# A one-core encoder layer: order of work in the opening, at three stage borders and in the last output tile

## Chip, core and metric

The kernel runs on one core of one Trainium2 chip. The metric is the device time of one execution in microseconds (us). Engines are called PE (matrix multiply; PEld is its weight load), DVE (vector), ACT (scalar), POOL (GpSimd) and SP (the queue that issues every DMA here). L331 is line 331 of the kernel before.

## What is computed

One layer of a bidirectional hybrid encoder on 1024 tokens plus 16 meta tokens, width 1024, all in float32:

```
h    = rmsnorm(concat(meta, x))
q,k,v,z,beta,a,scB,scC,scX,gateA,gateB = split(h @ w_in)      # 9248 columns
q,k,v = silu(conv5(q,k,v));  q,k l2-normalised per head       # 8 heads of 128
g    = -exp(A_log) * softplus(a + dt_bias)                    # log decays, per token, direction, head
o    = gated delta rule, chunks of 64, forward + backward     # needs cumulative sums of g
yA   = (rmsnorm(o) * silu(z)) @ w_branch_dn
yB   = (scB * conv3(scC * scX)) @ w_branch_sc
x    = h_in + (sigmoid(gateA) * yA + sigmoid(gateB) * yB) @ w_out
x    = x + (silu(gate) * up) @ w_down,  gate,up = rmsnorm(x) @ w_gate_up
out  = rmsnorm(x), meta tokens dropped
```

## The kernel before

**Products.** Every large product is taken in three parts: each operand is split into a high part (ACT casts it, L86) and a low part (DVE subtracts, L87), and PE adds high*high, high*low and low*high in one PSUM bank. So each new operand costs one ACT and one DVE instruction ahead of its matmuls. Eight PSUM banks are shared under three tags (m: 3, e: 2, d: 3).

**Opening and phase 1 (to about 1005 us).** This part runs in the order in which the source issues it; that order is partly written out by hand and partly dealt by a planner in the source with a model clock per engine (`T["pe"]`, `T["dve"]`, ...). Nine tiles of x are loaded, scaled (`root`, `scaled`, L1020) with the norm row `w1row`, turned on PE (`turned`, L83) and split (`highs`, `lows`). Between these steps the first two units of the input projection, `gen0` (K of head 0) and `gen1` (Q of head 0), are issued piece by piece: a unit is 128 columns of w_in against all tokens in three column chunks (`dense_steps`, L331), each chunk evicted by ACT (L387, L388) into a row buffer `ra` (two of them) for the convolution, which DVE does (`conv_job`, L354, L362, with a tanh on ACT, L359). A unit may evict into a row buffer only when the convolution of the unit two before it has read it. `small_gates` (L1051) multiplies the 32 columns of beta and a, whose split weights are `wba` (L1116 on ACT, L1118 on DVE). At the end of the opening the last pieces of `gen0` and `gen1` and the last `small_gates` are issued, and only then the last chunks of both units are evicted, the third unit (V of head 0) is picked and its weights are split in four pieces (`split_part`, L942 on ACT, L939 on DVE). From there the main loop goes on unit by unit and lets the planner put other work between the matmuls: `g_gates` (decays and their cumulative sums; the sums are matmuls with triangular constants, L1261), then per head `g_decay`, `g_norm`, `g_inv` and `g_scan` (the recurrence).

**Stages after it.** Here the compiler's scheduler deals instructions to the engine queues, among ready ones the earlier in the source first; matmuls of one step can so stand between those of another. The gate A, short-conv and DeltaNet projections are each done by `seven`: seven half-size products A to G of four operand steps, alternating between two sets of four banks, with copies or an eviction after a product. `halved` splits one operand step into one of four buffer pairs. For the DeltaNet branch the eviction (`evict_dn`) has three DVE instructions for each of four tiles when a kept part is added, two when none is; it leaves the merged rows `mg` (tiles mA and mB). `between` lists hold work hooked between the operand steps, among it `wo_row` (load and split one row tile of w_out). Then a loop over eight token tiles splits `mg` into `mh, ml` and multiplies with w_out (L1584 to L1586), adds x, normalises, and turns the tile one step late (`norm_T`). The feed-forward part prepares three units ahead (`stationary1`: load and split of gate and up columns; `part1`: first two products, L1644 to L1646), with `norm_T` of the last tile and `split_T2` between the second and the third.

**The end.** The down projection is again seven products, over 11 steps each. In the last one, five operand steps are kept back and done tile by tile, and `finish` normalises each tile and stores it. A late tile is stored in two halves: the high half scaled by ACT from `hiw`, the low half by DVE.

Of the kernel before, what the change touches and what calls it, by code (L numbers as in the profile page):

```python
# [8 lines left out]
F32 = mybir.dt.float32  # L9
# [7 lines left out]
P = 128  # L17
# [20 lines left out]
def encoder_layer(ctx: ExitStack, tc: tile.TileContext, x, meta, norm1_w, w_in,  # L38
# [26 lines left out]
    def psd():  # L65
        return ps.tile([P, 512], F32, tag="e", name=uid("pe"), bufs=2)
# [921 lines left out]
    with tc.tile_pool(name="st", bufs=1) as st:  # L988
# [29 lines left out]
        def scaled(t):  # L1018
            p = size(t)
            nc.vector.scalar_tensor_tensor(out=xs[t][:p], in0=xs[t][:p], scalar=rss[t][:p, 1:2], in1=w1row[:p],  # L1020
                                           op0=ALU.mult, op1=ALU.mult)
# [35 lines left out]
        def steps(g, n=KT):  # L1057
            for _ in range(n):
                next(g)
# [5 lines left out]
                transpose(idle[:, :P], ident)  # L1065

        load(0)
        load(1)
        nc.sync.dma_start(w1row, norm1_w[0:1, :].broadcast_to([P, D]))
        load(2)  # L1070
        u0 = pick()
        load(3)
# [41 lines left out]
        nc.scalar.copy(cols[:, :24], pt2[:, :24])  # L1114
        nc.scalar.mul(cols[:, 24:25], pt2[:, 24:25], 0.5)
        nc.scalar.copy(wba[:, :, 0:32], raw_ba)  # L1116
        scaled(3)
        nc.vector.tensor_tensor(out=wba[:, :, 32:64], in0=raw_ba, in1=wba[:, :, 0:32].bitcast(F32), op=ALU.subtract)  # L1118
        nc.scalar.copy(u1[1][0], u1[2])
        nc.gpsimd.tensor_tensor(out=u1[1][1], in0=u1[2], in1=u1[1][0].bitcast(F32), op=ALU.subtract)  # L1120
        root(4)
# [36 lines left out]
        lows(8, 0)  # L1158
        lows(8, 1)
        steps(gen0)  # L1160
        steps(gen1)
        small_gates(2)


# [27 lines left out]
    def g_gates():  # L1192
# [4 lines left out]
        nc.sync.dma_start(dtb, dt_bias.rearrange("a b c -> a (b c)").broadcast_to([P, 16]))  # L1197
        nc.sync.dma_start(alg, A_log.rearrange("a b c -> a (b c)").broadcast_to([P, 16]))
        nc.gpsimd.memset(BA, 0.0)
        pba = psd()  # L1200
        pbm = psd()
        for c in range(9):
# [33 lines left out]
        for k in (13, 11, 9, 7, 5, 3, 1):  # L1236
# [6 lines left out]
        nc.vector.tensor_scalar(out=alg, in0=alg, scalar1=-1.0, scalar2=None, op0=ALU.mult)  # L1243
        g = sr
        nc.vector.scalar_tensor_tensor(out=g, in0=a_, scalar=0.0, in1=sr, op0=ALU.max, op1=ALU.add)
        nc.vector.tensor_tensor(out=g, in0=g, in1=alg.unsqueeze(1).broadcast_to([P, 9, 16]), op=ALU.mult)
# [3 lines left out]
        nc.gpsimd.affine_select(out=g[:, 8, :], in_=g[:, 8, :], compare_op=ALU.is_gt, fill=0.0,  # L1250
                                base=META, pattern=[[0, 16]], channel_multiplier=-1)
        gcs = [c1.tile([P, 8, 9], F32, name=f"gc{d}") for d in range(2)]
        yield T["dve"] + 700
        for d in range(2):
            nc.vector.tensor_copy(gcs[d].rearrange("p h c -> p c h"), g[:, :, d * 8:d * 8 + 8])
            small_v()
        yield T["dve"] + TOPE
        for d in range(2):
            pt = psd().rearrange("p (a n) -> p a n", a=4)
            for i, m in enumerate((U2[d], U[d], E_[d], ones)):  # L1260
# [34 lines left out]
    for m_ in meta_inv:  # L1295
        nc.gpsimd.memset(m_, 0.0)
    SPL = (4, 6, 8, 10)
    for g in (gen0, gen1):
        for _ in g:
            pass  # L1300
    decs.append([g_gates(), T["pe"], None])
    ahead = [pick(), pick()]
    ahead[0][1] = wtiles([P, KT, P])
    while done < H or qkv_units or fill_units or any(ahead):
        u = ahead.pop(0)
        if u is None:
# [60 lines left out]
    def seven(pairs, X, Y, tok, evict, between, moving={}, snap=snap):  # L1367

        p1s = u2s = p5s = None
        for n, (key, bank, first) in enumerate((("A", X, True), ("B", Y, True), ("C", X, False), ("D", Y, True),  # L1370
                                                ("E", X, False), ("F", Y, False), ("G", X, False))):
            for f in between[n][0]:
                f()
            for k in range(4):
                h_, l_ = halved(pairs[key], k, 512 if key in moving else D)
                bh, bl = moving[key](k) if key in moving else (h_[:, hi], l_[:, hi])
                for t in range(4):
                    c = slice(t * P, t * P + P)
                    for j, (a, b) in enumerate(((h_, bh), (h_, bl), (l_, bh))):
                        fresh = first and k == j == 0  # L1380
                        mm(bank[t], a[:, c], b, start=fresh, stop=first and k == 3 and j == 2,  # L1381
                           skip_group_check=not first)
                for f in between[n][1 + k]:
                    f()
            if n in (0, 2, 3):
                keep_ = snap(n)
                for t in range(4):
                    nc.scalar.copy(keep_[t], bank[t])
                if n == 0:
                    p1s = keep_  # L1390
                elif n == 2:
                    u2s = keep_
                else:
                    p5s = keep_
            elif n == 6:
                evict(1, tok[0], bank, None)
            else:
                evict(*((0, tok[0], bank, p1s), (1, tok[1], bank, p5s), (0, tok[1], bank, u2s))[(1, 4, 5).index(n)])

    def p_block(dst, kh, half):  # L1400
# [144 lines left out]
    def wo_row(j):  # L1545
        raw = s4(D)
        nc.sync.dma_start(raw, w_out[j * P:j * P + P, :])
        split(*(t[:, j % 4] for t in wo[j // 4]), raw)

    during_dn = [  # L1550
        [[lambda: (new("G", "ah1"), w_part("G", 1, 1))], [lambda: by_two(add, L_(dn_, "D"), L_(dn_, "C"), L_(dn_, "A"))], [],
         [lambda: by_two(sub, R_(dn_, "D"), R_(dn_, "F"), R_(dn_, "C"))], []],
# [3 lines left out]
        [[lambda: wo_tiles(0, ("b0", "b3"))], [lambda: wo_row(0)], [lambda: wo_row(1)], [lambda: wo_row(2)], []],  # L1556
        [[], [lambda: wo_row(3)], [lambda: wo_tiles(1, ("b2", "b1"))], [lambda: wo_row(4)], []],
        none,
        [[], [], [lambda: wo_row(5)], [lambda: wo_row(6)], [lambda: wo_row(7)]]]
    seven(dn_, bank_m, bank_d, (1, 0), evict_dn, during_dn)  # L1560
    woh, wol = ([wo[j // 4][i][:, j % 4] for j in range(KT)] for i in range(2))
    rot["i"] = 4

# [8 lines left out]
    m32 = [m_[0][:, 0:2], m_[0][:, 2:4], m_[1], m_[2]]  # L1572
    m32 = [m.rearrange("p k i c -> p (k i) c") for m in m32]
    for t in range(KT):
        mh, ml = wtiles([P, KT, P])
        for i in range(2):
            split(mh[:, 4 * i:4 * i + 4], ml[:, 4 * i:4 * i + 4], mg[i][:, :, t * P:(t + 1) * P])
        xr = s4(D)
        nc.sync.dma_start(xr, x[t * P:(t + 1) * P])
        for n in range(2):  # L1580
# [104 lines left out]
    mov["T1"] = [[t1s[2 * i + k // 2][:, k % 2] for k in range(4)] for i in range(2)]  # L1685
    ahead = [part1(w0, sm[:, 0], sm[:, 2])]
    ahead.append(part1(stationary1(1), sm[:, 1], sm[:, 3]))
    norm_T(*late_norm)
    split_T2(slice(384, 512))
    p1_2 = [tp.tile([P, 512], F32, tag="t2", name=uid("t2"), bufs=2) for _ in range(2)]  # L1690
    ahead.append(part1(stationary1(2), *p1_2))
    u_hl[0] = big("w2", [P, 2, 4, P])
    block22(0, w0[1], w0[2])
    for n, i in (("T3", 3), ("T4", 2), ("B22", 0)):
# [97 lines left out]
    def finish(t):  # L1792
# [14 lines left out]
        nc.vector.scalar_tensor_tensor(out=r[:, lo], in0=r[:, lo], scalar=ss[:, 2:3], in1=wfr[:, lo], op0=ALU.mult, op1=ALU.mult)  # L1807
        nc.sync.dma_start(o_[:, lo], r[:, lo])

    half_ss = {}  # L1810
    for n, (a, b, bank) in enumerate((("A11", "B11", bank_x), ("A12", "B21", bank_y), ("S2", "T2", bank_x), ("S1", "T1", bank_y),
                                      ("S3", "T3", bank_x), ("S4", "B22", bank_y), ("A22", "T4", bank_x))):
        kept = []
        for k in range(HK):
            hl = operands(a, b, k)
            if n == 6 and k >= HK - NR:
                kept.append((k, hl))
                continue
            for t in range(4):
                tile_step(bank, hl, t, k == 0, k == HK - 1)  # L1820
        for t in range(4):
            for k, hl in kept:
                tile_step(bank, hl, t, False, k == HK - 1)
            u = us[:, t]
# [40 lines left out]
```

## Time and profile before

| what | before |
|---|---|
| time, median of 3 runs | 1990.61 us (1989.9 to 1991.65) |
| time of the profiled execution | 1991.52 us |
| its span, first to last instruction | 1989.5 us |
| PE busy | 1952.8 us, 98% |
| DVE busy | 1472.7 us, 74% |
| ACT busy | 868.1 us, 44% |
| POOL busy | 158.5 us, 8% |
| mean granted PE clock | 0.994 |

A busy share is a mean over stages with different limits. The list of PE's waits names every wait by the line that waited and the line that ended it; the view by stretches gives, for stretches of 5 us, the busy time of an engine and the granted clock as a share of full speed.

### The profile page before, as it was taken

To read this page: it belongs to the slowest core of one execution; us is meant where nothing else is said; L and a number is where in the kernel's file an instruction comes from. 1 tells how busy PE (TensorE), PEld (TensorE's weight loads), DVE (VectorE), ACT (ScalarE), POOL (GpSimd) and SP (SyncE) were. 2 spreads that over 40 slices of the span, in tenths; PEclk is the share of its full clock that TensorE was granted. 3 is DMA by queue.
4 is the path that set the end of the run, shared out by engine and by line. 5 is a ranking of instruction groups with operands and counts; after the bars stand their busy time and mean duration, and the time that the engine had idled before them with its cause. 6 is when DMAs were issued, how large, how long until landed. Compare 5 with 4: busy or idle time off the path is not lost.

```text
span 1989.5 us, 31925 instructions
## 1 busy us (share of the span) xinstructions
PE 1952.8 (98%) x11929; PEld 1709.9 (86%) x11929; DVE 1472.7 (74%) x2799; ACT 868.1 (44%) x2011; POOL 158.5 (8%) x455
## 2 busy tenths in 40 slices
PE   8899999999999999999999999999999999999998
PEld 7898899999999989998888888787888888888887
DVE  4687677888888888787348788559987777856574
ACT  5365435555555555442435545225332322325343
POOL 3002011111111211110000000000000000000001
PEclk9999999999999999999999999999999999999999
DMA  4123323132313131314377533232765445487554
GB/s 143 33 66 112 86 85 97 55 90 65 81 56 89 40 106 56 89 57 160 98 276 251 202 112 120 102 117 95 253 236 194 142 150 179 162 276 246 194 172 167
DMA packets 243279, 264.09 MB, mean 133 GB/s; under 512 B 46836, under 2 KB 166949, under 8 KB 240693
## 3 DMA queue, kind: packets, MB, share of 16 engines
q1 hardware_dynamic: 243125, 262.07, 40.5%
q8 instruction: 93, 1.52, 0.3%
q14 instruction: 61, 0.50, 0.1%
HBM read 189.58 MB, written 72.44 MB: 132 GB/s over the span
## 4 chain that ended last, share of the span: by engine, by line
PE 87%; DVE 8%; ACT 2%; DMA 1%; issue 1%; SPq 0%; POOLq 0%; DVEq 0%; POOL 0%; ACTq 0%
PE pm L331 29%; PE pm L1381 4%; PE pd L1381 4%; PE pm L1646 3%; PE pe L1381 3%; PE pm L1644 3%; PE pm L1645 3%; PE pd L1644 2%; PE pd L1646 2%; PE pd L1645 2%; DVE kq L354 2%; PE pe L1644 2%; PE pe L1646 2%; PE pe L1645 2%; PE pd L813 2%; PE pd L830 1%
## 5 line engine op out<-in xcount | busy, mean ns | idle before, releaser
L331 PE MATMUL pm<-hTh,wh 128*128 128x320 f32 (+4 forms) x1328 | 487.5, 368 | 2.8 <-ACT wh L942 2.8
L331 PE MATMUL pm<-hTh,wl 128*128 128x320 f32 (+4 forms) x1328 | 451.8, 341 | 0.0
L331 PE MATMUL pm<-al,wh 128*128 128x320 f32 (+4 forms) x1328 | 451.1, 341 | 0.5 <-DVE al L1045 0.5
L331 PEld LDWEIGHTS pm<-hTh,wh 128*128 128x128 f32 x1328 | 251.3, 189 | 17.3 <-ACT wh L942 3.1
L331 PEld LDWEIGHTS pm<-hTh,wl 128*128 128x128 f32 x1328 | 250.2, 189 | 15.7 <-DVE wl L939 0.2
L331 PEld LDWEIGHTS pm<-al,wh 128*128 128x128 f32 x1328 | 251.6, 190 | 13.2 <-DVE al L1045 0.7
L87 DVE TENSOR_TENSOR al<-raw,ring_h 128x1024 fp32r<-128x1024 f32 x73 | 88.3, 1223 | 64.6 <-ACT ring_h L86 64.3
L86 ACT CAST ring_h<-raw 128x1024 fp32r<-128x1024 f32 x73 | 76.6, 1053 | 104.4 <-PE pe L1787 36.7
L939 DVE TENSOR_TENSOR wl<-raw,wh 128x512 fp32r<-128x512 f32 x122 | 83.6, 686 | 34.5 <-ACT wh L942 34.3
L354 DVE SCALAR_TENSOR_TENSOR kq<-ra,wc,kq 128x520 f32<-128x520 f32 (+1 forms) x128 | 96.2, 752 | 10.5 <-ACT kq L388 7.8
L128 POOL TENSOR_SCALAR ss<-ss 128x1 f32<-128x1 f32 x12 | 4.1, 343 | 961.9 <-ACT b L1797 606.6
L494 DVE TENSOR_TENSOR fP<-fP,tm 128x135 f32<-128x135 f32 (+23 forms) x248 | 71.7, 289 | 7.2
L490 DVE TENSOR_TENSOR tm<-fP,fN 128x135 f32<-128x135 f32 (+23 forms) x248 | 72.1, 291 | 6.5
L942 ACT CAST wh<-raw 128x512 fp32r<-128x512 f32 x122 | 75.1, 617 | 1.4 <-PE pm L331 1.3
L820 ACT ACTIVATE w<-pd,small 128x128 f32<-128x128 f32 x128 | 40.2, 366 | 78.4 <-PE pd L813 69.6
L842 DVE SCALAR_TENSOR_TENSOR S<-S,eGl,pd 128x128 f32<-128x128 f32 x104 | 31.8, 344 | 54.7 <-PE pd L830 32.6
L87 DVE TENSOR_TENSOR raw<-pair,raw 128x1024 fp32r<-128x1024 f32 (+1 forms) x42 | 48.0, 1144 | 30.3 <-ACT raw L86 30.2
L86 ACT CAST raw<-pair 128x1024 fp32r<-128x1024 f32 (+1 forms) x42 | 41.7, 993 | 57.9 <-PE pd L1381 27.5
L87 DVE TENSOR_TENSOR wl<-pair,wh 128x1024 fp32r<-128x1024 f32 (+1 forms) x42 | 48.1, 1144 | 21.7 <-ACT wh L86 21.5
L1337 DVE TENSOR_TENSOR b<-pd,b 128x512 f32<-128x512 f32 x59 | 39.6, 686 | 30.2 <-PE pd L1646 30.1
L86 ACT CAST wh<-pair 128x1024 fp32r<-128x1024 f32 (+1 forms) x42 | 41.7, 992 | 46.2 <-PE pd L1381 24.9
L1337 DVE TENSOR_TENSOR b<-pm,b 128x512 f32<-128x512 f32 x58 | 39.1, 685 | 22.7 <-PE pm L1646 20.4
(643 smaller groups left out, 4932.8 us busy)
## 6 DMA issues: line engine op xcount, KB each, us to landing
raw<-in_w_in_dram SPq DMA_DIRECT2D x64, 512.0 KB
raw<-in_w_gate_up_dram SPq DMA_DIRECT2D x44, 512.0 KB
sums<-in_w_down_dram SPq DMA_DIRECT2D x22, 512.0 KB
t_d<-sums SPq DMA_DIRECT2D x11, 1024.0 KB
raw<-s_d SPq DMA_DIRECT2D x44, 256.0 KB
raw<-t_d SPq DMA_DIRECT2D x44, 256.0 KB
act_d<-b SPq DMA_DIRECT2D x43, 256.0 KB
raw<-act_d SPq DMA_DIRECT2D x33, 256.0 KB
```

Of the source, the lines that this page charges most:

```text
L86: nc.scalar.copy(hi, src)
L87: nc.vector.tensor_tensor(out=lo, in0=src, in1=hi.bitcast(F32), op=ALU.subtract)
L331: mm(po[:, :n], (wl if j == 2 else wh)[:, k], xl[k][:, t0:t0 + n] if j == 1 else xh[k][:, t0:t0 + n], start=(i == 0), stop=(i == 3 * KT - 1))
L354: nc.vector.scalar_tensor_tensor(out=acc, in0=raw[:, h0 + t:h0 + t + hn], scalar=wc[:, t, col:col + 1], in1=acc, op0=ALU.mult, op1=ALU.add)
L490: nc.vector.tensor_tensor(out=tv, in0=fP[:, 0:r, j:j + 1].broadcast_to([P, r, n]), in1=fN[:, j:j + 1, j + 1:32].broadcast_to([P, r, n]), o ...
L939: nc.vector.tensor_tensor(out=u[1][1][:, k], in0=u[2][:, k], in1=u[1][0][:, k].bitcast(F32), op=ALU.subtract)
L942: nc.scalar.copy(u[1][0][:, k], u[2][:, k])
L1337: add = lambda out, a, b: nc.vector.tensor_tensor(out=out, in0=a, in1=b, op=ALU.add)
L1381: mm(bank[t], a[:, c], b, start=fresh, stop=first and k == 3 and j == 2, skip_group_check=not first)
L1644: mm(po, ah[:, k], bhk, start=k == 0, stop=False)
L1645: mm(po, ah[:, k], blk, start=False, stop=False)
L1646: mm(po, al[:, k], bhk, start=False, stop=k == 3)
```

## The change

- Opening: the load of `w1row` is issued ahead of the second x tile's load. The low part of `wba` is taken ahead of `scaled(3)`. The last chunk of `gen0` is evicted right behind its matmuls; the third and fourth unit are picked there, and the third is split ahead of `gen1`'s last piece. The last chunk of `gen1` is evicted ahead of the last `small_gates`.
- `g_gates`: the product with the decay rates is written straight into the two tiles `gc` that the sums read (zeroed early on POOL), in four DVE instructions; the earlier single product, POOL's mask of the meta rows and two DVE copies go. The planner's wait ahead of the sums is shorter.
- DeltaNet branch: the four operand steps of the seventh product are split ahead of the sixth product's eviction. The first tile of the next loop is split (`out_tile`) ahead of the seventh product's steps, and the last three `wo_row` are hooked one step earlier.
- Feed-forward: the third `stationary1` stands ahead of `norm_T` of the last tile.
- End: the last tile's kept matmuls are done in two halves of 256 columns, each added and squared by itself; both output halves go into one row and out in one store.

```diff
         load(0)
+        nc.sync.dma_start(w1row, norm1_w[0:1, :].broadcast_to([P, D]))
         load(1)
-        nc.sync.dma_start(w1row, norm1_w[0:1, :].broadcast_to([P, D]))
...
+        nc.vector.tensor_tensor(out=wba[:, :, 32:64], in0=raw_ba, in1=wba[:, :, 0:32].bitcast(F32), op=ALU.subtract)
         scaled(3)
-        nc.vector.tensor_tensor(out=wba[:, :, 32:64], in0=raw_ba, in1=wba[:, :, 0:32].bitcast(F32), op=ALU.subtract)
...
         steps(gen0)
+        for _ in gen0:
+            pass
+        ahead = [pick(), pick()]
+        ahead[0][1] = wtiles([P, KT, P])
+        for k in range(4):
+            split_part(ahead[0], k)
         steps(gen1)
+        for _ in gen1:
+            pass
         small_gates(2)
...
+        gcs = [c1.tile([P, 8, 9], F32, name=f"gc{d}") for d in range(2)]
+        for gc in gcs:
+            nc.gpsimd.memset(gc, 0.0)
...
-        nc.vector.tensor_tensor(out=g, in0=g, in1=alg.unsqueeze(1).broadcast_to([P, 9, 16]), op=ALU.mult)
+        for d in range(2):
+            for c, p in ((slice(0, 8), P), (slice(8, 9), META)):
+                nc.vector.tensor_tensor(out=gcs[d][:p, :, c].rearrange("p h c -> p c h"), in0=g[:p, c, d * 8:d * 8 + 8],
+                                        in1=alg[:p, d * 8:d * 8 + 8].unsqueeze(1).broadcast_to([p, c.stop - c.start, 8]), op=ALU.mult)
...
-        nc.gpsimd.affine_select(out=g[:, 8, :], in_=g[:, 8, :], compare_op=ALU.is_gt, fill=0.0,
-                                base=META, pattern=[[0, 16]], channel_multiplier=-1)
-        gcs = [c1.tile([P, 8, 9], F32, name=f"gc{d}") for d in range(2)]
-        yield T["dve"] + 700
-        for d in range(2):
-            nc.vector.tensor_copy(gcs[d].rearrange("p h c -> p c h"), g[:, :, d * 8:d * 8 + 8])
-            small_v()
-        yield T["dve"] + TOPE
+        yield on("dve", 500) + TOPE
...
-    for g in (gen0, gen1):
-        for _ in g:
-            pass
     decs.append([g_gates(), T["pe"], None])
-    ahead = [pick(), pick()]
-    ahead[0][1] = wtiles([P, KT, P])
...
-                h_, l_ = halved(pairs[key], k, 512 if key in moving else D)
+                h_, l_ = ready.pop(0) if ready else halved(pairs[key], k, 512 if key in moving else D)
...
             else:
+                if last_first and n == 5:
+                    ready = [halved(pairs["G"], k, D) for k in range(4)]
                 evict(*((0, tok[0], bank, p1s), (1, tok[1], bank, p5s), (0, tok[1], bank, u2s))[(1, 4, 5).index(n)])
...
+    def out_tile():
+        t = len(out_tiles)
+        mh, ml = wtiles([P, KT, P])
+        for i in range(2):
+            split(mh[:, 4 * i:4 * i + 4], ml[:, 4 * i:4 * i + 4], mg[i][:, :, t * P:(t + 1) * P])
+        out_tiles.append((mh, ml))
...
-        [[], [], [lambda: wo_row(5)], [lambda: wo_row(6)], [lambda: wo_row(7)]]]
-    seven(dn_, bank_m, bank_d, (1, 0), evict_dn, during_dn)
+        [[out_tile, lambda: wo_row(5)], [], [lambda: wo_row(6)], [lambda: wo_row(7)], []]]
+    seven(dn_, bank_m, bank_d, (1, 0), evict_dn, during_dn, last_first=True)
...
     for t in range(KT):
-        mh, ml = wtiles([P, KT, P])
-        for i in range(2):
-            split(mh[:, 4 * i:4 * i + 4], ml[:, 4 * i:4 * i + 4], mg[i][:, :, t * P:(t + 1) * P])
+        if t:
+            out_tile()
+        mh, ml = out_tiles[t]
...
+    third = stationary1(2)
     norm_T(*late_norm)
     split_T2(slice(384, 512))
     p1_2 = [tp.tile([P, 512], F32, tag="t2", name=uid("t2"), bufs=2) for _ in range(2)]
-    ahead.append(part1(stationary1(2), *p1_2))
+    ahead.append(part1(third, *p1_2))
...
+    def finish_last(bank, kept):
+        r, o_ = rows[7], out[7 * P:8 * P]
+        c = slice(3 * P, 4 * P)
+        ss = keep.tile([P, 4], F32, tag="ss3", name=uid("ss3"), bufs=2)
+        for i in range(2):
+            q = slice(256 * i, 256 * i + 256)
+            qh = slice(512 + 256 * i, 768 + 256 * i)
+            for k, (h_, l_) in kept:
+                for a_, b_ in ((h_, h_), (h_, l_), (l_, h_)):
+                    mm(bank[:, q], a_[:, c], b_[:, qh], start=False, stop=False, skip_group_check=True)
+            add(r[:, q], bank[:, q], r[:, q])
+            nc.scalar.activation(junk[:, D + 256 * i:D + 256 * i + 256], r[:, q], AF.Square, scale=RD, accum_out=ss[:, i:i + 1])
+            if i == 0:
+                nc.gpsimd.tensor_tensor(out=ss[:, 0:1], in0=ss[:, 0:1], in1=half_ss[7], op=ALU.add)
+        rsqrt(ss[:, 2:3], ss[:, 1:2], ss[:, 0:1])
+        nc.scalar.activation(r[:, hi], hiw[:, 3 * 512:4 * 512], AF.Copy, scale=ss[:, 2:3])
+        nc.vector.scalar_tensor_tensor(out=r[:, lo], in0=r[:, lo], scalar=ss[:, 2:3], in1=wfr[:, lo], op0=ALU.mult, op1=ALU.mult)
+        nc.sync.dma_start(o_, r)
```

More of the change, by code (lines that the diff above doesn't have):

```diff
@@ L1365, in snap, with seven @@
         return [keep_[:, t] for t in range(4)]
-    def seven(pairs, X, Y, tok, evict, between, moving={}, snap=snap):
+    def seven(pairs, X, Y, tok, evict, between, moving={}, snap=snap, last_first=False):
         p1s = u2s = p5s = None
+        ready = []
         for n, (key, bank, first) in enumerate((("A", X, True), ("B", Y, True), ("C", X, False), ("D", Y, True),
@@ L1548, in wo_row @@
         split(*(t[:, j % 4] for t in wo[j // 4]), raw)
+    out_tiles = []
+    def out_tile():
[4 more added lines that the diff above has]
+        out_tiles.append((mh, ml))
     during_dn = [
@@ L1819, in encoder_layer @@
             for t in range(4):
-                tile_step(bank, hl, t, k == 0, k == HK - 1)
+                tile_step(bank, hl, t, k == 0, k == HK - 1 or (n == 6 and t == 3 and k == HK - NR - 1))
         for t in range(4):
+            if n == 6 and t == 3:
+                finish_last(bank[t], kept)
+                break
             for k, hl in kept:
```

## The prediction, made before the changed kernel ran

> **What bounds the kernel now.** I read the page's busy shares first, then the list of PE's waits, then stretches of 5 us for the granted clock, then each engine's instructions around every wait.
>
> ```profile
> PE 1952.8 (98%) x11929; PEld 1709.9 (86%) x11929; DVE 1472.7 (74%) x2799; ACT 868.1 (44%) x2011; POOL 158.5 (8%) x455
> PE pd L813 <- DVE r L805: 6.5, 5, 1.6
> PE pe L1261 <- DVE gc L1255: 2.9, 1, 2.9
> PE pm L331 <- ACT wh L942: 2.8, 1, 2.8
> PE pm L1646 <- DVE wl L87: 2.7, 1, 2.7
> PE pe L1051 <- DVE wba L1118: 2.7, 1, 2.7
> PE pd L83 <- DVE xr L1020: 2.4, 1, 2.4
> PE pd L1586 <- DVE wl L87: 2.0, 1, 2.0
> PE pd L1584 <- ACT wh L86: 1.3, 2, 0.8
> ```
>
> PE bounds nearly all of the span, so only time in which PE waits or runs slowly can be won. The change aims at seven of these eight rows (not L813): the opening's L83, L1051, L331 and L1261, the border to the w_out loop (L1584, L1586), the border to the feed-forward part (L1646). A wait also costs what comes behind it. In the stretches (second column PE busy, then, in the first fence, the granted clock) the clock falls behind all but one of the long waits:
>
> ```profile
> 20.00:25.00 5.00, 2.27 (x15) 1.00 0.89 233
> 55.00:60.00 5.00, 2.24 (x11) 0.90 0.00 0
> 60.00:65.00 5.00, 5.00 (x23) 0.50 0.42 111
> 65.00:70.00 5.00, 5.00 (x33) 0.92 0.01 2
> 75.00:80.00 5.00, 5.00 (x35) 1.00 0.30 86
> 100.00:105.00 5.00, 5.00 (x27) 0.66 0.36 105
> ```
> ```profile
> 1250.00:1255.00 5.00, 2.95 (x10) 2.04 (x9) 5.00 (x10) 0.00 (x0) 0.00 (x0) 0.86 0.06 18
> 1255.00:1260.00 5.00, 5.00 (x19) 4.01 (x18) 2.33 (x5) 0.00 (x0) 0.00 (x0) 0.79 0.01 3
> 1360.00:1365.00 5.00, 2.51 (x7) 1.99 (x8) 5.00 (x7) 3.56 (x5) 0.00 (x0) 0.79 0.00 0
> 1365.00:1370.00 5.00, 5.00 (x21) 4.06 (x20) 4.75 (x7) 1.46 (x3) 0.00 (x0) 0.87 0.58 213
> ```
>
> In the second fence the clock is the number ahead of the last two. Lost to it, as (1 - clock) x 5 us: 0.5 + 2.5 + 0.4 = 3.4 us behind the L331 wait, 1.7 behind L1261, 0.7 + 1.05 = 1.75 behind L1586, 1.05 + 0.65 = 1.7 behind L1646. Together 8.55 us.
>
> [...]
>
> **The change part by part.** *wba.* ACT has the high part early; DVE's low part takes 2.56 us beside a POOL subtraction, where an instruction of the same width elsewhere (the L1212 row) takes 0.42:
>
> ```profile
> 17.81 0.41 ACT L1116 CAST wba<-wba_raw 128x256 fp32r<-128x256 f32 x1
> 20.25 2.56 DVE L1118 TENSOR_TENSOR wba<-wba_raw,wba 128x256 fp32r<-128x256 f32 x1
> 19.25 3.28 POOL L1120 TENSOR_TENSOR wl<-raw,wh 128x1024 fp32r<-128x1024 f32 x1 [0.23 <-ACT wh L1119]
> 64.13 0.42 DVE L1212 TENSOR_TENSOR BA<-pe,BA 128x256 f32<-128x256 f32 x1
> ```
>
> Moved ahead of `scaled(3)` it can start at 17.81 + 0.41 = 18.2 and, at 0.42, ends before POOL starts at 19.25; PE wants it at 20.25 + 2.56 - 2.7 = 20.1. The wait of 2.7 goes. What is needed next, u1's low part, ends at 19.25 + 3.28 = 22.5, while PE still does the 24 instructions of `small_gates(0)` and `turned(3)`; at 0.143 each (35 in 5 us, slice 75 to 80) they last to 23.5: hidden, with about 1 us to spare. Gain 2.7 (ends 1.5 and 2.7); no clock falls here.
>
> *w1row ahead of the second tile.* Both loads are equal in size. The first tile can be scaled sooner, the second later, by at most the 2.4 us that PE waited. ACT and DVE then join both; I take 0, ends -0.9 and +0.7.
>
> *Third unit.* Its split waits for ACT to evict four chunks behind the last `small_gates`, though ACT and DVE had stood idle for 9.82 and 13.71 us:
>
> ```profile
> 56.55 0.47 ACT L1055 COPY baT<-pe 64x384 f32<-64x384 f32 x1 [9.82 <-PE pe L1051]
> 58.61 1.14 ACT L942 CAST wh<-raw 128x512 fp32r<-128x512 f32 x2
> 59.26 1.29 DVE L939 TENSOR_TENSOR wl<-raw,wh 128x512 fp32r<-128x512 f32 x2 [13.71 <-ACT wh L942]
> 18.08 4.86 SPq L932 DMA_DIRECT2D raw<-in_w_in_dram x2
> ```
>
> Behind `gen0`'s last piece, ACT's 1.14 and DVE's 1.29 lie beside `gen1`'s piece and `small_gates(2)` on PE. The picks are two more DMAs, but SP passes them no other queue entry and had issued both by 18.08 + 4.86 = 22.9 us. The wait of 2.8 and its 3.4 of clock go: 6.2. The transposes of `baT` then come sooner behind ACT's 0.47 us copy; a few tenths, in the remainder below.
>
> *Decays.* DVE makes the product, POOL masks it, and the two copies stand far behind on DVE, behind convolution work, which waits for ACT:
>
> ```profile
> 92.69 0.31 DVE L1246 TENSOR_TENSOR sr<-sr,alg 128x144 f32<-128x144 f32 x1
> 93.07 0.74 POOL L1250 TENSOR_SCALAR_AFFINE_SELECT sr<-sr 128x16 f32<-128x16 f32 x1 [8.83 <-DVE sr L1246]
> 97.51 0.41 ACT L387 COPY ra<-pm 128x322 f32<-128x322 f32 x1
> 99.50 0.33 DVE L1255 COPY gc<-sr 128x72 f32<-128x72 f32 x2
> ```
>
> Four small products in place of one cost at most 4 x 0.31 - 0.31 = 0.9 more on DVE and save 0.33 of copies and POOL's 0.74 off the path. `gc` is then ready by about 94, before PE comes to it (the copies end at 99.50 + 0.33 = 99.8, less the wait of 2.9: 96.9). Wait and clock, 2.9 + 1.7 = 4.6, go. What is late next is a PSUM bank: the chunk evicted at 97.51 is the first of three, it waits for the convolution two units back, and PE wants its bank again after the third chunk. DVE's chain moves up by less than PE does (PE also wins the clock), so I charge a wait of 1.1 (ends 0 and 2.9). POOL's two memsets are off the path: POOL is 8% busy.
>
> *Border to w_out.* DVE runs without a gap from the eviction at 1234.27; the split of the third G step comes behind all twelve of its instructions, that of the first `mg` tile behind the next eviction too:
>
> ```profile
> 1234.27 0.68 DVE L1337 TENSOR_TENSOR snap<-pe,snap 128x512 f32<-128x512 f32 x1
> 1242.61 1.22 DVE L87 TENSOR_TENSOR raw<-pair,raw 128x1024 fp32r<-128x1024 f32 x1
> 1251.97 0.68 DVE L87 TENSOR_TENSOR wl<-mA,wh 128x512 fp32r<-128x512 f32 x1
> ```
>
> With the two late G splits ahead (2 x about 1.14), the first eviction ends some 2.3 us later, near 1243.8; the `mg` split follows by 1245.5, and PE, whose F ends about 1 us into the eviction, ends G's 48 matmuls of 0.23 (price below) near 1246.2 if it need not wait. The last eviction, eight instructions of at most 0.68, then lies beside the first tile's matmuls. The waits, 2.0 + 1.3, and 1.75 of clock go: 5.05 (ends 2 and 5.5). One later cover: a w_out row whose buffer the eviction frees comes 2.3 us later, about as much as it has to spare.
>
> *Border to feed-forward.* ACT had the third unit's high part ten microseconds before DVE made the low part:
>
> ```profile
> 1351.46 1.06 ACT L86 CAST wh<-raw 128x1024 fp32r<-128x1024 f32 x1
> 1361.22 1.22 DVE L87 TENSOR_TENSOR wl<-raw,wh 128x1024 fp32r<-128x1024 f32 x1
> 1364.63 0.68 DVE L87 TENSOR_TENSOR mA<-al,mA 128x512 fp32r<-128x512 f32 x1
> ```
>
> Ahead of `norm_T` it runs near 1353; 2.7 + 1.7 = 4.4 go. `stationary1` issues two loads on SP; `norm_T` and `split_T2` issue none that they could delay. What is late next: DVE is full here, and the first product of the main loop, needs T2's last quarter (1364.63 + 0.68 = 1365.3). PE stood from 1361.22 + 1.22 - 2.7 = 1359.7 with 20 of the third unit's 24 matmuls to do; at 0.23 it would now come to T2 at 1364.3. I charge 1.0 (ends 0 and 2.5).
>
> *Last tile.* Before, 15 matmuls of 512 columns at 0.23 each; then the chain:
>
> ```profile
> 1982.14 0.24 PE pe L1787
> 1982.40 0.70 DVE mA L1337
> 1983.18 0.63 ACT L1802 ACTIVATE b<-mA 128x512 f32<-128x512 f32 x1 [0.87 <-DVE mA L1337]
> ```
>
> Now 30 of 256 columns. The narrowest near form, mostly 320 columns, runs at those 0.143: 30 x 0.143 - 15 x 0.23 = +0.8 at most, nothing if 256 columns cost half of 512. The add falls to about 0.42 and the square by about 0.25: -0.5. One store saves an issue but sends the high half with the low one. If the second half must wait until DVE has read the bank, 0.4 to 0.6 more. I take 0 (ends -0.8 and +1.4).
>
> *The remainder.* The planner's DVE clock and one of its waits change, so the order after 60 us is dealt anew; before it held 6.5 us of L813 waits. I charge 1.0 for this and the `baT` wait (ends -4 and +5).
>
> **Sum.** Waits 2.7 + 2.8 + 2.9 + 3.3 + 2.7 = 14.4; clock 8.55; given back 1.1 + 1.0 + 1.0 = 3.1. 14.4 + 8.55 - 3.1 = 19.85. The profiled execution took 1991.52 us (span 1989.5 and 2.0 around it), so 1971.7. The median of the runs is 0.9 below it: 1990.61 - 19.85 = 1970.8.
>
> **Rivals.** *The borders stay.* The scheduler deals those stages by what it thinks is ready; it might leave the splits where they are. It already put L1584 matmuls among G's. Then 5.05 + 4.4 - 1.0 = 8.45 are lost: 1979.2. Against: DVE is full there, so the source's order decides.
>
> *The clock falls anyway.* If the low stretches are not these waits' doing, they stay: 1970.8 + 8.55 = 1979.3. For it: the wait in the slice from 20 us brought none. Against: each of the four begins at a wait. [...]
>
> *DVE holds the opening.* The convolution chain, not PE, sets when banks come free, and takes back the decays' gain and the third unit's clock, 4.6 - 1.1 + 3.4 = 6.9: 1977.7. For it: the eviction at 97.51.
>
> *Slower: a worse deal.* The scan has 8 heads x 8 steps; each waits at L813 on DVE, now five times, 1.6 at the longest. Were the new order to make each of the 64 wait 0.4 more, 25.6 come back: 1970.8 + 25.6 = 1996.4. From 19.85 / 64 = 0.31 per step it is slower. Against: the planner's rules are unchanged, and DVE starts earlier.
>
> **How the numbers follow.** The forecast as worked out 0.60, borders 0.12, clock 0.08, DVE 0.12, a worse deal 0.05, and 0.03 for mishaps near no change. A change of 0.2% is 4.0 us, about what a measurement of this kernel tells from none. Faster by more: the first four, 0.92; within: 0.04 (mishaps and a small bad deal); slower: 0.04. The forecast's own ends: 1964 if nothing is given back and the deal is kind, 1976 with every give-back at its upper end. The range takes in the three rivals near 1979: 1964 to 1980.5.
>
> **What would show it.** Right: PE's waits lose L1261, L331 on L942, L1051, L1586 and L1646, and the clock stays at 1.00 from 50 to 110, 1245 to 1260 and 1360 to 1370; L939 starts before 52; `gc` is written before 95; the G splits stand before the eviction. Wrong: new waits of PE on ACT L387 near 90, on DVE mA near 1364, or more than 10 us at L813; low clock without a wait.

## The result and the profile after

The changed kernel takes 1980.12 us (median of 5 runs, 1978.99 to 1981.91). The kernel before, run beside it on the same chip, takes 1991.65 us. The ratio is 0.9939 (95% interval 0.9925 to 0.9953): 11.5 us faster there, and 10.5 us below the 1990.61 from which the forecast of 1970.8 started. The time lies inside the range, 0.4 us from its slow end, and above the forecast's own ends (1964 to 1976). The profiled execution took 1981.91 us, its span is 1980.1 us, so 9.4 us less than before, where the sum promised 19.85.

The busy shares, and the list of PE's waits (total, how many, longest, in us):

```profile
PE 1949.2 (98%) x11944; PEld 1705.7 (86%) x11944; DVE 1471.3 (74%) x2801; ACT 868.0 (44%) x2013; POOL 159.2 (8%) x457
PE pd L813 <- DVE r L805: 6.1, 5, 1.6
PE pe L1834 <- DVE mA L1338: 2.0, 1, 2.0
PE pd L713 <- issue: 1.9, 1, 1.9
PE pm L1799 <- ACT ring_h L86: 1.8, 1, 1.8
PE pe L1267 <- DVE gc L1259: 1.2, 1, 1.2
PE pe L1659 <- DVE s_hl L87: 1.1, 1, 1.1
PE pm L1659 <- DVE wl L87: 0.9, 1, 0.9
PE pe L1657 <- ACT s_hl L86: 0.8, 1, 0.8
```

Of the rows that the change aimed at, those for `wba`, for the third unit in the opening and for the w_out border are gone; that for tiles of x (L83 on `xr`) is still 2.4, now in three pieces. The wait for `gc` has fallen from 2.9 to 1.2, that for the third feed-forward unit's `wl` from 2.7 to 0.9. New are a wait in the last tile (L1834) and two for `s_hl`. L713 and L1799 (L1785 in before) stood at 0.9 and 0.8 us before.

The stretches in which the clock had fallen (the granted clock is the third number from the end):

```profile
20.00:25.00 5.00, 5.00 (x37) 4.49 (x36) 1.70 (x2) 2.40 (x5) 3.39 (x5) 1.00 0.94 220
55.00:60.00 5.00, 5.00 (x35) 5.00 (x34) 3.81 (x9) 1.34 (x4) 0.00 (x0) 1.00 0.02 5
60.00:65.00 5.00, 5.00 (x32) 5.00 (x31) 3.55 (x6) 2.23 (x7) 0.13 (x2) 1.00 0.00 2
95.00:100.00 5.00, 5.00 (x36) 5.00 (x35) 4.50 (x8) 1.17 (x5) 0.00 (x0) 1.00 0.09 20
1236.00:1241.00 5.00, 5.00 (x22) 3.58 (x21) 4.40 (x6) 2.21 (x4) 0.00 (x0) 1.00 0.99 311
1241.00:1246.00 5.00, 5.00 (x24) 4.14 (x23) 5.00 (x10) 0.00 (x0) 0.00 (x0) 1.00 0.27 102
1345.00:1350.00 5.00, 4.41 (x19) 3.68 (x20) 5.00 (x7) 3.87 (x5) 0.00 (x0) 1.00 0.00 0
```

These stretches are all at full clock; the half clock that is left lies at L713, in the down projection and in the last tile. The steps moved as the diff says. Opening and w_out border, ACT and DVE by time:

```profile
17.42 0.43 DVE L1117 TENSOR_TENSOR wba<-wba_raw,wba 128x256 fp32r<-128x256 f32 x1 [0.31 <-ACT wba L1116]
47.48 1.14 ACT L942 CAST wh<-raw 128x512 fp32r<-128x512 f32 x2
48.13 1.29 DVE L939 TENSOR_TENSOR wl<-raw,wh 128x512 fp32r<-128x512 f32 x2 [5.56 <-ACT wh L942]
83.67 0.51 DVE L1259 TENSOR_TENSOR gc<-sr,alg 128x64 f32<-128x64 f32 x4
1237.10 0.69 DVE L87 TENSOR_TENSOR wl<-mA,wh 128x512 fp32r<-128x512 f32 x1 [0.60 <-ACT wh L86]
1237.70 2.35 DVE L87 TENSOR_TENSOR b<-s,b 128x1024 fp32r<-128x1024 f32 x2
1239.97 1.28 DVE L1514 SCALAR_TENSOR_TENSOR s<-s,pm 128x512 f32<-128x512 f32 x2
```

`wba`'s low part takes 0.43 instead of 2.56 us, the third unit's splits start 11 us sooner, and the `mg` split (1237.10) stands ahead of the last eviction (1239.97).

**Where the time came from.** Every matmul of before was paired with the same one of the changed kernel (same source line, same count), and the median difference of their starts read near each border. A minus is earlier:

| stage | forecast | changed | changed, second trace |
|---|---|---|---|
| opening and scan, to 905 us of before | -11.4 | -11.6 | -11.1 |
| L713 near 912 | 0 | +2.6 | +0.7 |
| border to w_out | -5.05 | -6.0 | -6.1 |
| border to feed-forward, to 1400 | -3.4 | +0.2 | +0.2 |
| down projection, near 1786 | 0 | +2.65 | +0.2 |
| last tile, to the end of the span | 0 | +2.9 | +2.0 |
| sum | -19.85 | -9.4 | -14.1 |

(Forecast of the opening: 2.7 + 6.2 + 3.5 - 1.0. The second trace is of the fifth run below. Differences under 0.1 between the rows are left out.) Opening and w_out border paid about as forecast, the feed-forward border and the last tile did not, and two places that the change does not touch cost 5.2 us in one trace and 0.9 in the other. The lines that the two losses show are in the next section, beside the runs that take them apart.

### The profile page after: what moved, and what is told of

It is laid out like the page before. It is cut to its first block, busy times and chain, and to the rows that moved or that the text cites. A ratio compares the mean times of both kernels' runs of the same rounds, so it can differ in the third digit from the quotient of the medians.

```text
span 1980.1 us, 31950 instructions
## 1 busy us (share of the span) xinstructions
PE 1949.2 (98%) x11944; PEld 1705.7 (86%) x11944; DVE 1471.3 (74%) x2801; ACT 868.0 (44%) x2013; POOL 159.2 (8%) x457
## 4 chain that ended last, share of the span: by engine, by line
PE 89%; DVE 7%; ACT 2%; DMA 1%; issue 1%; SPq 0%; POOL 0%; POOLq 0%; DVEq 0%; ACTq 0%
PE pm L331 31%; PE pm L1383 5%; PE pd L1383 4%; PE pe L1383 3%; PE pm L1659 3%; PE pm L1657 3%; PE pm L1658 3%; PE pd L1657 2%; PE pd L1658 2%; PE pd L1659 2%; DVE kq L354 2%; PE pe L1659 2%; PE pe L1657 2%; PE pe L1658 2%; PE pd L813 2%; PE pd L830 1%
## 5 line engine op out<-in xcount | busy, mean ns | idle before, releaser
L354 DVE SCALAR_TENSOR_TENSOR kq<-ra,wc,kq 128x520 f32<-128x520 f32 (+1 forms) x128 | 96.3, 752 | 10.2 <-ACT kq L388 7.8
```

The source lines that it names most:

```text
L354: nc.vector.scalar_tensor_tensor(out=acc, in0=raw[:, h0 + t:h0 + t + hn], scalar=wc[:, t, col:col + 1], in1=acc, op0=ALU.mult, op1=ALU.add)
```

## The experiments

The theory at the outset: waits and their low clock are won where they go; the shortfall is three things, a bank wait in the last tile, DVE's order at the feed-forward border, and waits that differ from run to run. The rivals are that the clock, or DVE as the bound, takes the gain back.

**1. The last tile as before.** In the changed kernel, DVE and then PE in the last tile:

```profile
1969.32 0.75 DVE L1821 SCALAR_TENSOR_TENSOR mA<-mA,ss,w 128x512 f32<-128x512 f32 x1 [1.89 <-POOL ss L130]
1969.98 0.42 DVE L1338 TENSOR_TENSOR mA<-pe,mA 128x256 f32<-128x256 f32 x1
```
```profile
1968.21 0.28 PE L1834 MATMUL pe<-ring_h,al 128*128 128x256 f32 x1
1970.46 0.39 PE L1834 MATMUL pe<-ring_h 128*128 128x256 f32 x1 [1.97 <-DVE mA L1338]
1971.04 0.28 PE L1834 MATMUL pe<-al,ring_h 128*128 128x256 f32 x1
1971.85 0.41 PE L1834 MATMUL pe<-ring_h 128*128 128x256 f32 x1
```

The first half's last matmul starts at 1968.21, but DVE's add (1969.98) stands behind its scaling of the tile ahead (1969.32), which waits for POOL. The next matmul into the bank starts at 1970.46, behind that add's end (1969.98 + 0.42 = 1970.40). From 1971.4 on, about 1 us behind the wait, the matmuls stand 0.21 instead of 0.12 us apart.

```diff
-            if n == 6 and t == 3:
-                finish_last(bank[t], kept)
-                break
```

> The changed kernel with its last tile put back: 15 matmuls of 512 columns, one add, one square, two stores. Against the changed kernel's 1980.1 us. Theory (the halves share a bank, so the second half's matmuls wait until DVE has read the first half): the wait of 1.97 us at the second half and the 0.21 instead of 0.12 us per matmul behind it go; PE ends 3.2 us sooner, the tail behind it is 7.1 again instead of 6.7, so 1977.3 us (1976.5 to 1978). Rival (the loss at the end comes from the tile ahead, whose scaling DVE does late, and would meet one whole add just as much): 1980 +- 0.5 us.

Measured: 1976.23 us, ratio to before 0.9916 (0.9901 to 0.9931). The last stage is 0.0 against before, instead of +2.9. The whole add meets the same late scaling at no cost, so the rival falls.

**2. The halves in two banks.**

```diff
+        add(r[:, lo], bank, r[:, lo])
...
+            ho = halves2[i][:, 0:256]
-                    mm(bank[:, q], a_[:, c], b_[:, qh], start=False, ...)
+                    mm(ho, a_[:, c], b_[:, qh], start=x == y == 0, ...)
-            add(r[:, q], bank[:, q], r[:, q])
+            add(r[:, q], ho, r[:, q])
```

> The changed kernel with the last five steps of the last tile's halves in two other banks, free by then; what the old bank holds is added to the row once, early (one more add of 512 columns, 0.7 us on DVE). Theory (bank wait): the second half's matmuls follow at 0.12 us without a wait, PE ends near 1970.1 in the profiled run instead of 1973.3, the second add starts when DVE is through with the first, near 1970.6 instead of 1973.4: 1977.3 us (1976.7 to 1978). Rival 1 (DVE's late scaling of the tile ahead sets the end): 1978.5 to 1980. Rival 2 (it is not the bank but the clock or the half width): the wait of 1.97 stays, 1980 +- 0.5.

Measured: 1975.9 us, 0.9913 (0.9897 to 0.9928); the last stage is -0.1. No wait is left in the last tile and its matmuls stay 0.12 us apart. So that the halves share a bank is the cause, together with DVE's late add, which no run moved ahead of the scaling. (A bank is one tile of this program, so the runs don't tell a guard by bank from one by tile.) Halving by itself is worth about nothing: the forecast's 0.5 for the shorter add and square is not seen. With the add as late as here the shared bank cost a wait of 1.97 us, and two banks do without it.

**3. The feed-forward border put back.**

```diff
-    third = stationary1(2)
     norm_T(*late_norm)
     split_T2(slice(384, 512))
...
-    ahead.append(part1(third, *p1_2))
+    ahead.append(part1(stationary1(2), *p1_2))
```

> The changed kernel with the third unit of the feed-forward part split behind norm_T and T2's last quarter again, as before; all else as changed. Theory (DVE is the bound in this border: the 3.4 us that the earlier split gains are given back within 18 us, because the deal pulls three subtractions of the down weights' sums ahead of s_hl): the wait of 2.7 and its low clock return (3.4 us), the deal falls as before, and the time stays at 1980 +- 0.7 us. Rival (the later waits come from the earlier parts and not from this move): they stay beside the old wait, so 1983.5 us (1982.8 to 1984.2).

Measured: 1977.79 us, 0.9921 (0.9907 to 0.9936). The wait of 2.75 and a clock of 0.66 (1345 to 1350) are back, the two waits for `s_hl` are gone, and the border comes out at +0.1 against before, as with the move (+0.2). The move gains 3.4 us by the third unit's end and pays them back within 18 us.

**4. Who pays it back.** DVE, then PE, of the changed kernel:

```profile
1344.32 1.22 DVE L87 TENSOR_TENSOR wl<-raw,wh 128x1024 fp32r<-128x1024 f32 x1
1358.68 0.69 DVE L141 TENSOR_TENSOR sums<-sums 128x512 f32<-128x512 f32 x1
1360.48 0.70 DVE L141 TENSOR_TENSOR sums<-sums 128x512 f32<-128x512 f32 x1
1364.68 0.70 DVE L141 TENSOR_TENSOR sums<-sums 128x512 f32<-128x512 f32 x1
1366.48 1.24 DVE L87 TENSOR_TENSOR s_hl<-raw,s_hl 128x1024 fp32r<-128x1024 f32 x1
```
```profile
1365.91 0.50 PE L1657 MATMUL pe<-s,s_hl 128*128 128x512 f32 x1 [0.80 <-ACT s_hl L86]
1367.77 0.50 PE L1659 MATMUL pe<-s,s_hl 128*128 128x512 f32 x1 [1.13 <-DVE s_hl L87]
```

Three subtractions for the down projection's weights (`sums`), which nothing needs for 400 us, stand ahead of the second unit's `s_hl`, for which PE waits. In before they came behind it:

```profile
1379.58 1.23 DVE L87 TENSOR_TENSOR s_hl<-raw,s_hl 128x1024 fp32r<-128x1024 f32 x1
1383.17 0.69 DVE L141 TENSOR_TENSOR sums<-sums 128x512 f32<-128x512 f32 x1
```

The edit holds the first of them back:

```diff
-    def down_sums(k):
+    def down_sums(k, late=None):
...
+        if late is not None:
+            for i in range(2):
+                nc.scalar.copy(r[:, i, 0:1], late[:, 0:1])
...
-            down_sums(j - 1)
+            down_sums(j - 1, u2 if j == 1 else None)
```

> The changed kernel with the first down weights' sums made to wait for the end of the second unit (a one-column copy of that unit's last result into their buffer ahead of their load), so that DVE does the second unit's s_hl ahead of them. It adds two ACT copies and about 0.2 us of ACT. Theory (three subtractions of 0.7 us stand ahead of s_hl and PE waits 0.8 + 1.1 us for it): both waits go, 1978.2 us (1977.3 to 1978.7). Theory that DVE is full whatever the order: s_hl is late by less, but b's and T's splits or the next unit's wait in its place: 1979.5 to 1980.5. Rival (s_hl waits for the load or for PE's own products): no change, 1980.1 +- 0.4, and the sums just move.

Measured: 1976.95 us, 0.9919 (0.9904 to 0.9934); the border is now -1.35 instead of +0.2. Of that kernel, DVE's row and the only wait for `s_hl` that is left:

```profile
1364.03 1.22 DVE L87 TENSOR_TENSOR s_hl<-raw,s_hl 128x1024 fp32r<-128x1024 f32 x1
PE pm L1657 <- ACT s_hl L86: 0.6, 1, 0.6
```

So 1.5 of the 3.6 us that were given back are the `sums`. (The two ACT copies took 0.19 us each.) The other 2.1 stay, and here the theory that DVE is full fits: in this kernel it is busy for 37.3 of the 38 us from 1334 to 1372 (37.6 in the changed kernel). But the waits that PE still has behind the third unit, 0.3 for `b` and 0.6 for `s_hl`, are only 0.9 of the 2.1, and no run took work off DVE, so this part is argued and not shown.

All four runs so far came out 0.3 to 1.5 us below the ranges expected for their theories, though before, beside them, took 1993.99 us. The shifts by stage decide between the readings here, not the single times.

**5. The changed kernel once more, and before once more.** No edits.

> The changed kernel as it is, on the chip of the runs beside it. Theory (of the changed kernel's first trace, PE's wait of 1.88 us near 902 and of 1.83 us near 1772, with the low clock behind them, 2.6 us each, are the run's own): at least one of the two is shorter here, the opening shows -11 +- 0.5 us against before, the w_out border -6.1 +- 0.2, the feed-forward border +0.2 +- 0.2, the last tile +2.85 +- 0.2. Rival (they belong to the change): both waits are again over 1.5 us with low clock behind them. Time 1977.5 to 1980.5 us.

> The kernel before as it is, for a second trace of it. Theory (two waits of PE, of 0.93 us near 912 and 0.79 us near 1786, and the clock behind them, differ from run to run): at least one of them differs by over 0.4 us from the first trace, and every other stage agrees within 0.4 us. Rival: all stages agree, and the two waits with them.

Measured: 1978.69 us, 0.993 (0.9914 to 0.9945), and for before 1995.13 us in a single run. The changed kernel's wait near 1772 was 0.9 instead of 1.8 us and brought no low clock; L713's was 1.6 and cost 0.7 instead of 2.6. Two rows of the second trace of before:

```profile
PE pm L331 <- issue: 1.4, 1, 1.4
PE pd L713 <- issue: 1.4, 1, 1.4
```

The first of them (at 819.66) is not in the first trace at all and shifts all that follows by 1.6 us. So the length of these waits, and whether the clock falls behind them, changes from run to run. But my expectation that all else would agree within 0.4 us missed too: the feed-forward border of before took 1.3 us longer behind the same wait (2.74): half clock lasted 6.8 us there, instead of 3.4. The last tile was +2.0 instead of the expected +2.85, since the clock here held 1.00 behind the same wait of 1.97; over seven traces with halves in one bank it cost 2.0 to 3.5 us.

**6. Two parts put back, 1200 us apart.**

```diff
         load(0)
-        nc.sync.dma_start(w1row, norm1_w[0:1, :].broadcast_to([P, D]))
         load(1)
+        nc.sync.dma_start(w1row, norm1_w[0:1, :].broadcast_to([P, D]))
...
-    seven(dn_, bank_m, bank_d, (1, 0), evict_dn, during_dn, last_first=True)
+    seven(dn_, bank_m, bank_d, (1, 0), evict_dn, during_dn)
```

(with the hooks of `during_dn` and `out_tile` as before.)

> The changed kernel with two parts put back that lie 1200 us apart, so that each is read in its own stage: w1row's load behind the second tile's, and the splits at the border to the w_out loop behind the evictions. Theory: w1row is worth 0 +- 0.5 us by 30 us into the span; the w_out border loses 6.1 us (waits 3.3, low clock 1.75, and about 1 of smaller gaps), which the later stages do not give back: 1979.5 + 6.1 = 1985.6 us (1984.5 to 1987). Rival for the border (DVE is the bound there too, and the later border gives back what this one gained): 1980 to 1983. Rival for w1row: its move brought 0.8 us or more.

Measured: 1985.63 us, 0.9966 (0.9954 to 0.9978), 6.9 above the changed kernel beside it. By 30 us the shift is -3.2 against -3.0 and -2.8 in the changed kernel's two traces: `w1row` is worth nothing. The w_out border gives 0.0 instead of -6.1, with its waits and its low clock back:

```profile
PE pd L1596 <- ACT wh L86: 1.3, 2, 0.8
1240.00:1245.00 5.00, 2.95 (x8) 2.24 (x8) 5.00 (x9) 0.00 (x0) 0.00 (x0) 0.76 0.00 0
1245.00:1250.00 5.00, 5.00 (x21) 4.11 (x20) 2.13 (x4) 0.00 (x0) 0.00 (x0) 0.90 0.01 3
```

**7. The opening's two larger parts put back, one at a time.**

```diff
-        for d in range(2):
-            for c, p in ((slice(0, 8), P), (slice(8, 9), META)):
-                nc.vector.tensor_tensor(out=gcs[d]..., in0=g..., in1=alg..., op=ALU.mult)
+        nc.vector.tensor_tensor(out=g, in0=g, in1=alg.unsqueeze(1).broadcast_to([P, 9, 16]), op=ALU.mult)
...
+            nc.vector.tensor_copy(gcs[d].rearrange("p h c -> p c h"), g[:, :, d * 8:d * 8 + 8])
```

> The changed kernel with the decays put back: one product, POOL's mask, two late copies. Theory (wait and low clock, 2.9 + 1.7 us, come back, and the new wait of 1.2 us for the four small products goes): the opening gives 3.4 us less by 130 us into the span, 0.5 to 1 of which the deal returns: -8.3 +- 0.7 there instead of -10.9; 1981.5 us beside the 1978.7 of the changed kernel. Rival (DVE holds the opening: PE meets the convolution chain later anyway): -10 or more there, 1979 to 1980. Rival (the low clock was not the wait's doing): -9.9 to -9.3.

```diff
-        for _ in gen0:
-            pass
-        ahead = [pick(), pick()]
-        ahead[0][1] = wtiles([P, KT, P])
-        for k in range(4):
-            split_part(ahead[0], k)
         steps(gen1)
-        for _ in gen1:
-            pass
```

(the picks and the last chunks' evictions stand behind the last small gates again.)

> The changed kernel with the opening's third unit put back behind the last small gates. Theory (the wait of 2.8 us and the low clock of 3.4 behind it return): -4.7 +- 0.7 us by 130 us into the span instead of -10.9, 1984.8 us (1983.8 to 1986). Rival (DVE holds the opening and takes the clock's part back at the decays): -7 to -8. Rival (the clock falls for another reason): -8.

Measured, first without the new decays: 1985.18 us, 0.9954 (0.994 to 0.9968); -8.4 by 130 us as expected, and -7.2 by 360, where the changed kernel has -11.2 and -11.0. Then without the third unit's early split: 1983.55 us, 0.9945 (0.9933 to 0.9958), a little under the range expected; -5.1 by 130 us. The rows, of the first and of the second kernel:

```profile
PE pe L1269 <- DVE gc L1263: 3.7, 1, 3.7
90.00:95.00 5.00, 3.73 (x20) 3.73 (x21) 3.90 (x8) 2.62 (x9) 0.00 (x0) 0.78 0.37 105
95.00:100.00 5.00, 5.00 (x33) 4.99 (x33) 3.24 (x8) 1.34 (x5) 0.00 (x0) 0.87 0.04 11
```
```profile
PE pm L331 <- ACT wh L942: 2.8, 1, 2.8
55.00:60.00 5.00, 3.47 (x20) 2.92 (x21) 3.53 (x6) 2.81 (x7) 0.00 (x0) 0.88 0.23 61
60.00:65.00 5.00, 5.00 (x28) 5.00 (x28) 3.81 (x9) 0.64 (x1) 0.00 (x0) 0.78 0.20 53
```

Each wait comes back with its low clock. The third unit is worth 5.4 to 5.8 us, the decays 2.1 by 130 us and about 4 after the deal; why the deal widens this, where the expectation had it give some back, is open. The first kernel's time is 3.7 us above the expected 1981.5: besides the opening, its trace lost 1.5 us near 1113 (PE waits 1.3 us for a DVE split), 1.8 at the feed-forward border and 3.5 in the last tile. DVE does not hold the opening.

**8. Better versions.** The last tile as before together with the `sums` behind `s_hl`; then two banks with the `sums`; then that with PE's sums over the decays asked for 1.5 us later:

```diff
-        yield on("dve", 500) + TOPE
+        yield on("dve", 500) + TOPE + 1500
```

> The changed kernel with the last tile as before and the first sums behind the second unit's s_hl. Theory (both losses are separate): 2.85 + 1.5 = 4.4 us under the changed kernel run beside it, about 1974.5 us (1973 to 1976); against before, by stage, opening -11, w_out border -6.1, feed-forward border -1.3, last tile 0: 18.4 in all. Rival (one loss hides the other, as the tail waits on DVE): 1976 to 1977.5.

> The changed kernel with the last tile's halves in two banks and the first sums behind s_hl. Theory (halving in two banks is worth 0 to 0.2 us against one whole add): the same as the whole tile with the sums behind, 1974.4 +- 0.7 us; last tile 0 +- 0.2 against before. Rival (one store and halves bring the forecast's 0.5): 1973.7 and -0.5 in the last stage.

> The kernel of the run before (two banks, sums behind s_hl) with the sums over the decays put 1.5 us later in the planner's clock, so that PE does 12 more matmuls of 320 columns (1.7 us) ahead of them. Theory (PE comes to gc 1.2 us too early only because the planner expects DVE's four products 1.2 us too soon): the wait of 1.2 us goes, -12 us instead of -10.9 by 130 us into the span, 1973.2 us. Rival (what DVE owes there is owed later: the convolution's banks): -10.9 +- 0.3 and no gain; the deal behind it may move either way by 0.5.

Measured: 1974.4 us, 0.9906 (0.9889 to 0.9923); 1976.2 us, 0.9906 (0.9893 to 0.992), beside a slower before (1994.4 against 1992.03); 1977.85 us, 0.9915 (0.9901 to 0.9928). The first two are equal and the best: the first lies 4.3 us under the changed kernel run beside it, about the 2.85 + 1.5 expected. The second's trace lost 2.6 us at L713 and 1.5 near 1113, where the first's lost 1.1 and nothing. The third did lose the `gc` wait (-11.3 by 130 us), but had -10.2 by 360 and came out 4.6 us above the expected 1973.2: as its rival said, what DVE owed there was owed later (PE's waits for DVE's `PQ` at L582 are 2.0 instead of 1.3 us in all).

## Why the prediction was right, and where it was not

The direction and the larger half of the sum were right, term by term:

- *wba* (2.7): -3.0 by 30 us; a second trace of before differs by 0.3 from the first there. *w1row* (0): nothing, as taken; other waits for x tiles (2.4 in three pieces) stand where 2.4 stood in one.
- *Third unit* (6.2): 5.4 to 5.8. *Decays* (4.6 less 1.1): 2.1 to 4.0. The give-back was placed wrongly: no bank was late, but `gc` itself (1.2), because the planner now deals the sums sooner than DVE has the four products. The sizes met by luck.
- *Border to w_out* (5.05): 6.0 to 6.1. The waits counted, 3.3, leave out one of 0.4 at L1381 (for a DVE split), and behind three of the waits there the second matmul comes 0.34 us after the first instead of 0.23 (1243.88 to 1244.22, 1249.46 to 1249.80 and 1252.70 to 1253.04 in before).
- *Border to feed-forward* (3.4 net): the step that failed is the charge of 1.0 us (ends 0 and 2.5) for what is late next. The 3.4 us did come, and 3.6 went. I looked for the next operand in the order of the source and found T2; the scheduler takes ready work, and pulled the `sums` ahead of `s_hl`. That DVE is full here was in the prediction, as an argument that the source's order holds.
- *Last tile* (0, ends -0.8 and +1.4): the step that failed is "if the second half must wait until DVE has read the bank, 0.4 to 0.6 more". The wait is 1.97, since DVE's add is queued behind the scaling of the tile ahead, and the low clock behind it makes 2.0 to 3.5. The matmuls of 256 columns themselves cost half of 512 (0.12 against 0.23).
- *The remainder* (1.0): the deal took nothing; from 130 to 905 us the changed kernel's two traces gain 0.9 and 0.6 more, and L813 is 6.1 instead of 6.5. That the opening's sum of 11.4 was met by 11.6 and 11.1 is luck too, since its terms were off both ways.

The forecast's own upper end was summed too low: 1976 counts the give-backs of the decays, the feed-forward border and the last tile at their ends (1.8 + 1.5 + 1.4 above what was charged), but not the remainder's, with which it is 1979.5. The 5.2 us that the first trace lost at L713 and in the down projection are in no term at all. The range reaches the measured time only through the room given to the three rivals near 1979, and none of them was the case: the splits at the borders moved, the clock rose, and DVE did not hold the opening. So that the time lies inside the range is luck; the direction is not, nor are the gains in the opening and at the w_out border, which runs 6 and 7 took apart. With the last tile mended and 1.5 us of the feed-forward border won back, the best version's trace is 17.7 us under before, 1.7 us of losses at L713 and in the down projection included.

PE stands at L713 for 0.9 to 2.0 us in all 14 traces, 0.9 and 1.4 in before's two, and the list names no engine that it waits for ("issue"). Ahead of the wait matmuls of 32x32 follow each other about every 0.01 us. The traces do show something there: packets of 16 KB on a DMA queue marked `instruction`, 94 of them in the changed kernel and 93 in before. One of them starts at 899.56 in the changed kernel, where PE stands from 900.07 to 901.95, and one at 910.30 in before, where PE goes on at 912.59: 2.4 and 2.3 us behind the packet's start, for waits of 1.88 and 0.93. That PE waits for what the packet brings would be a guess; no run tested it. Why the wait is longer in some runs, and whether the change lengthens it (1.0 to 2.0 in twelve traces), stays open.

## What to carry to other kernels

Where the engine that feeds the bottleneck is full, moving one piece of its work ahead only picks who is late next (here 3.4 us were won and 3.6 given back): list all that is ready there, in its own order, useless early work included, and hold that back. Two halves of a result in one bank made no pipeline here (a wait of 1.97 us, and none with two banks): ask what stands in the queue of the engine that must read the first half. And compare stages by the same instruction in both traces, since single runs of one kernel differ by as much as a part of a change is worth (the changed kernel's five by 2.9 us).

## What the runs showed of the chip that was not expected

Equal waits did not always cost the same here: the clock behind them fell in one run and not in another. At L713, the changed kernel (wait 1.9) and then the best version (wait 2.0):

```profile
900.00:905.00 5.00, 3.12 (x32) 2.49 (x24) 2.06 (x3) 1.94 (x5) 0.00 (x0) 0.80 0.05 16
905.00:910.00 5.00, 5.00 (x47) 3.84 (x46) 4.28 (x5) 1.21 (x3) 0.00 (x0) 0.86 0.48 193
```
```profile
900.00:905.00 5.00, 3.03 (x27) 2.49 (x28) 2.06 (x3) 2.54 (x6) 0.00 (x0) 1.00 0.05 15
905.00:910.00 5.00, 5.00 (x72) 3.85 (x72) 4.88 (x5) 0.62 (x2) 0.00 (x0) 1.00 0.60 242
```

The first lost 2.6 us there, the second 1.1. At the feed-forward border the same two waits for `s_hl` (0.8 and 1.1) brought no low clock in the changed kernel, but 0.73 (1370 to 1375) in the run without the w_out part and 0.78 in the one without the decays, where that border gave +1.7 and +1.8 instead of +0.2. The prediction counted the clock as surely as the wait; behind waits of 1.9 to 2.0 us it fell in some of these runs and not in others.

In the traces of before and of the changed kernel half clock lasts 3.41 us at a time ahead of the last tile, once 6.83 (from 58.98 in before); by an estimate from the halved clock such a fall costs 1.7 or 3.4 us. The instants at which the recorded clock changes lie whole multiples of 3.413 us apart in each of these two traces (in the changed kernel 902.97, 906.38, 1773.37, 1776.78 and 1971.34). The same two waits, in stretches of that length (PE busy, then the clock), the changed kernel first:

```profile
899.56:902.97 3.41, 1.53 (x69) 1.00 0.19 71
902.97:906.38 3.41, 3.41 (x9) 0.50 0.14 50
```
```profile
897.24:900.65 3.41, 2.70 (x90) 1.00 0.87 288
900.65:904.07 3.42, 2.10 (x23) 1.00 0.02 8
```

The first wait lies whole in one stretch, in which PE is busy for 45%, and half clock follows; the second lies across two, with 79% and 61%, and none follows. In the stretch ahead of the changed kernel's two other falls PE is busy for 44% (from 1769.96) and 42% (from 1967.93), ahead of the four falls of before that the prediction counts for 28% (from 55.57), 15% (96.53), 40% (1250.24) and 20% (1359.46). The wait of 2.7 us at 20 us in before, which the prediction left as an exception, lies across two stretches (62% from 18.02 and 58% from 21.44), and no fall follows. So in these cases the fall went with how little PE did in one stretch, more than with the length of the wait. No run moved a wait to test this, and what sets the clock is not shown.
